# Attention of a hybrid encoder: sample values by pairs, a new split of the copies of turned weights, and a shorter opening

## The chip, the cores and the metric

The kernel runs on one core of one Trainium2 chip. The metric is the device time of one execution in microseconds (us). The core has a matrix engine (TensorE, called PE in the profile), a vector engine (VectorE, DVE), a scalar engine (ScalarE, ACT), a general engine (GpSimd, POOL) and a queue engine (SyncE, SP) that here only issues transfers. Matmuls write into PSUM banks, from which VectorE and ScalarE read. Every engine works through its own list of instructions in order; where one needs another's result, it waits.

## The reference

Two layers over 640 tokens: one new stream of 512 frames (the prompt) and eight running streams with 16 new frames each (the samples). All data are float32. A layer is a gated feed-forward step, a mixer (short convolution and attention from one common projection, merged by two gates) and a second feed-forward step.

```python
x += 0.5 * swiglu(rmsnorm(x, norm_ffn1), w_ffn1_gu, w_ffn1_down)
z = rmsnorm(x, norm_mix) @ w_in            # conv B, C, V | q, k, v | two gates
y_conv = B * causal_conv3(C * V)
y_attn = softmax(q k^T / 8 + rel_bias, banded by chunks of 64) v     # 8 heads of 64
m = sigmoid(g_c) * (y_conv @ w_conv_out) + sigmoid(g_a) * (y_attn @ w_attn_out)
x += m @ w_o
x += 0.5 * swiglu(rmsnorm(x, norm_ffn2), w_ffn2_gu, w_ffn2_down)
```

For the prompt the attention is 512 by 512, with the part above the diagonal of chunks left out. For each sample the 16 new frames read 256 cached keys and values and their own 16. The outputs are the final norm of all tokens and the new keys, values and convolution rows.

## The kernel before

Activations lie with channels on the partitions and 640 tokens along the free axis, in two halves of 320. Each float32 product of a weight matrix is three matmuls of 320 columns: weights and activations are split into a rounded part (whi, hhi, thi) and the rest (wlo, hlo, tlo), and hi x hi, hi x lo and lo x hi are summed in PSUM. The weights stream in as tiles of 512 KB (raw, by SyncE); ScalarE casts each to whi, VectorE subtracts to get wlo, and three buffers of each kind go round.

The opening of the first feed-forward step (`opening`, L620) begins with `stir`: matmuls of a constant tile (ones) whose result nobody reads. TensorE runs them while the first tokens and weights arrive. Each of them has float32 operands and leaves two rows in the trace.

In `attention` the products that turn queries, keys, gates and convolution inputs out of h are handed out as a stream: `fill(n)` runs the next n pieces of it, six matmuls of 320 columns each, and the small matmuls of attention stand between. The prompt's attention takes heads in four passes of two (e = 0 and 1). A pass computes scores (pss), and `softmax` (exponentials on ScalarE, L1943) and `weigh` (scaling on ScalarE, L1801) give the weights. `values` then transposes them on TensorE block by block: for each column block j = 0 to 3, and for each of the two heads, the transposes of `turn` (L1814) write a PSUM tile ptp of 512, 384, 256 or 128 columns, and one copy (L1817) moves it to pt in SBUF, on VectorE for e = 0 and on ScalarE for e = 1. Six transposes stand in the second half of each pass: two of j = 2 for each head and one of j = 3 for each.

The samples come after that. `sscores(b)` loads the cached keys (kc), the cached values (vc) and the new values (vn) of sample b by SyncE, has GpSimd add the 16 new keys, and runs the scores on TensorE (spss, L1872) in strips of 32 columns of the array, one strip for each pair of heads. VectorE adds the bias and takes the maximum (L1879) into a box, and softmax follows. `svalues(b)` has three parts: three transposes of the box (sptp, L1895 and L1896) and their copies on ScalarE and VectorE; then the values (spy, L1906), again in strips of 32 columns, first the new ones with 16 rows (vn) and then the cached ones in two blocks of 128 rows (vc), and a scaling on ScalarE (L1908); then one transpose of the result (ptx, L1912). After every fourth sample the collected results are copied to yas. The box of a sample is a tile of the ring "pt", in use from its scores to its ptx; the scores of b + 2 are written while b is being worked on.

What sets the order: each engine takes its instructions as the code is written, except that those under `soon()` are put forward by up to 300 instructions. PSUM tiles made by `att` go round one set of banks, so that a new tile waits until the tile that had its bank has been read.

Of the kernel before, what the change touches and what calls it, by code (L numbers as in the profile page):

```python
# [10 lines left out]
F32 = mybir.dt.float32  # L11
F32R = mybir.dt.float32r
AF = mybir.ActivationFunctionType
# [167 lines left out]
def trunk(ctx: ExitStack, tc: tile.TileContext, xin, xtok, wst, small, pbias, samplebias, kcache, vcache,  # L181
# [27 lines left out]
    def att(name):  # L209
        return banks["att"].tile([P, 512], F32, tag="att", name=name)  # L210
# [154 lines left out]
    def soon():  # L365
        return tc.high_priority(offset=300)
# [42 lines left out]
    def stir(ps, n):  # L409
        for _ in range(n):  # L410
            PE.matmul(ps[:, :P], ones, ones, start=True, stop=True)
# [203 lines left out]
    def opening(fp, name, goff, n, put, tails):  # L615
# [1 line left out]


        ACT.copy(early, epst)
        stir(att(f"stir{name}"), 15)  # L620
        ex = Expand(fp, name, goff)
        ex.ps = fp.tile([P, NT], F32, name=f"sums{name}", bufs=1)
        load(2)
# [1060 lines left out]
    def attention(l, h, norms, stats, ops, mp, yas, ycp, both, others):  # L1684
# [119 lines left out]
        def values(p):  # L1804

            pt = [mp.tile([P, offs[-1] + SEQ], F32, name=f"pt{l}_{2 * p + e}", tag="pt") for e in range(2)]
            at = [sum(P * (NQ - i) for i in range(j)) for j in range(NQ)]

            def turn(j, e):
                w = (NQ - j) * P  # L1810
                s = weights[2 * p + e]
                ptp = att(f"ptp{l}_{2 * p + e}_{j}")[:, :w]
                for i in range(j, NQ):
                    PE.transpose(ptp[:, (i - j) * P : (i - j + 1) * P],  # L1814
                                 s[:, offs[i] + j * P : offs[i] + (j + 1) * P], ident)
                with soon():
                    (ACT.copy if e else DVE.tensor_copy)(pt[e][:, at[j] : at[j] + w], ptp)  # L1817

            for j in range(NQ):
                for e in range(2):  # L1820
                    turn(j, e)
                if j % 2:
                    yield
            py = att(f"py{l}_{p}")
            for j in range(NQ):
                for e in range(2):
                    hh = 2 * p + e
                    PE.matmul(py[e * HD : (e + 1) * HD, j * P :], vs[j][:, hh * HD : (hh + 1) * HD],
                              pt[e][:, at[j] : at[j] + (NQ - j) * P], start=j == 0, stop=j == NQ - 1)
            ACT.copy(yas[:, p, 0:SEQ], py)  # L1830
            yield
# [17 lines left out]

        sbias = mp.tile([P, KS], F32, name=f"sbias{l}", bufs=1)  # L1850
        POOL.dma_start(sbias, samplebias[l])
        G = 4
        held, ptx = {}, [None]

        def sscores(b):
            n = f"{l}_{b}"
            kcs = []
            for e, tag in enumerate("qk"):
                kc = mp.tile([P, T], F32, name=f"kc{n}_{e}", tag=tag)
                kcs.append(kc[:, : npair // 2 * KS].rearrange("p (a k) -> p a k", k=KS))  # L1860
                SP.dma_start(kcs[e][:, :, :PAST], kcache[l, b, :, e * npair // 2 : (e + 1) * npair // 2])
            vraw = mp.tile([P, offs[-1] + SEQ], F32, name=f"vc{n}", tag="s")
            vraw = vraw[:, : 2 * AW].rearrange("p (a k) -> p a k", a=2)
            SP.dma_start(vraw, vcache[l, b])
            rows = slice(b * TS, (b + 1) * TS)
            vn = mp.tile([P, SEQ], F32, name=f"vn{n}", tag="bias")[:TS, :AW]
            SP.dma_start(vn, vnew[rows])
            for e, kc in enumerate(kcs):
                POOL.tensor_copy(kc[:, :, PAST:], ks[:, e * npair // 2 : (e + 1) * npair // 2, rows])
            pss = att(f"spss{n}")[:, :KS]  # L1870
            for p in range(npair):
                PE.matmul(pss[32 * p : 32 * p + 32], bd[:, b, p, :], kcs[2 * p // npair][:, p % (npair // 2), :],  # L1872
                          start=True, stop=True)

            box = mp.tile([P, offs[-1] + SEQ], F32, name=f"ss{n}", tag="pt")
            s = box[:, :KS]
            st = mp.tile([P, 4, NQ], F32, name=f"sst{n}", tag="st", bufs=4)
            with soon():
                DVE.tensor_tensor_reduce(out=s, in0=pss, in1=sbias, scale=1.0, scalar=NEG,  # L1879
                                         op0=ALU.add, op1=ALU.max, accum_out=st[:, 0, 0:1])  # L1880

                softmax(s, st, [(0, KS)])
                if b == NB - 1:
                    ACT.activation(early, st[:, 3, 0:1], AF.Sigmoid)
            held[b] = box, st, vraw, vn

        def svalues(b):
            n = f"{l}_{b}"
            box, st, vraw, vn = held[b]
            s = box[:, :KS]  # L1890
            pt = box[:, KS : KS + 2 * P].rearrange("p (a b) -> p a b", a=2)
            pn, yx = (box[:n, KS + o * P : KS + (o + 1) * P] for n, o in ((TS, 2), (P, 3)))
            ptp = att(f"sptp{n}")
            for j in range(2):
                PE.transpose(ptp[:, j * P : (j + 1) * P], s[:, j * P : (j + 1) * P], ident)  # L1895
            PE.transpose(ptp[:TS, 2 * P : 3 * P], s[:, PAST:], ident)  # L1896
            with soon():
                ACT.copy(pt, ptp[:, : 2 * P].rearrange("p (a b) -> p a b", a=2))
                DVE.tensor_copy(pn, ptp[:TS, 2 * P : 3 * P])
            yield  # L1900

            pys = att(f"spy{n}")[:, :P]
            for j, (w, v) in enumerate(((pn, vn), (pt[:, 0], vraw[:, 0]), (pt[:, 1], vraw[:, 1]))):
                for p in range(npair):
                    r = slice(32 * p, 32 * p + 32)
                    PE.matmul(pys[r], w[:, r], v[:, p * P : (p + 1) * P], start=j == 0, stop=j == 2)  # L1906
            with soon():
                ACT.activation(yx, pys, AF.Copy, scale=st[:, 3, 0:1])  # L1908
            yield
            if b % G == 0:  # L1910
                ptx[0] = att(f"ptx{n}")
            PE.transpose(ptx[0][:, (b % G) * P : (b % G + 1) * P], yx, ident)  # L1912
            if b % G == G - 1:
                c0 = SEQ + (b + 1 - G) * TS
                for e in range(2):
                    r = slice(e * HD, (e + 1) * HD)
                    with soon():
                        (ACT.copy if e else DVE.tensor_copy)(
                            yas[r, :, c0 : c0 + G * TS].rearrange("p a (b t) -> p a b t", b=G),
                            ptx[0][r].rearrange("p (b a e t) -> p a b e t", b=G, a=npair, e=2)[:, :, :, e, :])  # L1920

        sscores(0)
        sscores(1)
        for b in range(NB):
            vals = svalues(b)
            fill(4)
            next(vals)
            fill(3)
            if b + 2 < NB:
                sscores(b + 2)  # L1930
            next(vals)
            fill(2)
            next(vals, None)
        fill(KT * KT)

    def softmax(s, st, parts):
# [307 lines left out]
```

## Time and profile before

| | |
|---|---|
| median of 3 runs | 2493.01 us (2492.5 to 2493.15) |
| profiled execution | 2492.73 us, its span 2490.9 us |
| granted TensorE clock, mean | 0.999 |
| PE busy | 2481.3 us |
| DVE busy | 2115.8 us |
| ACT busy | 1443.3 us |
| POOL busy | 370.3 us |
| HBM | 223.75 MB read, 7.94 MB written |

The profile is of one execution. Busy times are of each engine, and a share is against the span. In a timeline row the first number is the start in us from the start of the span, the second the length of the group, then engine, source line, operation, what it writes and reads, its form and how many instructions were merged into the row; a bracket names an idle time ahead of it and what ended it. The start of one row to the start of the next is the step in which the engine moves on; the length of a matmul is longer than its step, since matmuls overlap. The prompt's and the samples' attention of layer 0 lie between about 490 and 640 us, those of layer 1 about 1232 us later.

### The profile page before, as it was taken

How to read it: one execution, taken by the hardware profiler on the slowest of the kernel's cores; microseconds unless marked ns; L12 is line 12 of the kernel's file. 1: busy time of each engine (PE TensorE's matmuls, PEld its weight loads, DVE VectorE, ACT ScalarE, POOL GpSimd, SP SyncE). 2: the span in 40 equal slices, each digit the busy share in tenths (PEclk: the TensorE clock that was granted, in tenths of full speed). 3: DMA queues.
4: the chain of work that ended last, by engine and by line, in shares of the span. 5: the costliest groups of instructions: out<-in, count | busy, mean ns of one | idle time of the engine just before them, and what ended most of it. 6: DMA issues, size and time to landing. Idle time of an engine off the chain costs nothing.

```text
span 2490.9 us, 43594 instructions
## 1 busy us (share of the span) xinstructions
PE 2481.3 (100%) x17084; PEld 2424.0 (97%) x17084; DVE 2115.8 (85%) x3327; ACT 1443.3 (58%) x2340; POOL 370.3 (15%) x445
## 2 busy tenths in 40 slices
PE   9999999999999999999999999999999999999998
PEld 9999999888999999999999999998899999999998
DVE  7789888878888899888798889888788888989887
ACT  6445556664666555555555555556646665555554
POOL 0011211111111011111001111121111110111111
PEclk9999999999999999999999999999999999999999
DMA  5244654335345344555435554643344553454554
GB/s 188 82 115 125 137 136 130 108 106 173 102 111 152 98 117 119 134 135 135 117 92 129 130 130 121 138 119 118 127 151 105 125 140 95 119 133 122 130 136 111
DMA packets 134990, 310.74 MB, mean 125 GB/s; under 512 B 12960, under 2 KB 76832, under 8 KB 134784
## 3 DMA queue, kind: packets, MB, share of 16 engines
q1 hardware_dynamic: 70704, 221.80, 26.4%
q0 software_dynamic: 63360, 85.50, 20.5%
q8 instruction: 134, 2.20, 0.4%
q10 hardware_dynamic: 720, 0.65, 0.1%
q14 instruction: 72, 0.59, 0.1%
HBM read 223.75 MB, written 7.94 MB: 93 GB/s over the span
## 4 chain that ended last, share of the span: by engine, by line
PE 95%; DVE 3%; ACT 2%; issue 0%; DVEq 0%; POOL 0%; ACTq 0%; POOLq 0%
PE pab L395 12%; PE paa L395 11%; PE pcb L395 6%; PE pca L395 6%; PE daa L1077 5%; PE dab L1077 5%; PE po L372 4%; PE qa L395 4%; PE pbb L395 3%; PE pba L395 3%; PE dcb L1077 3%; PE dca L1077 3%; PE poa L372 2%; PE pda L372 2%; PE pv L1737 2%; PE ma_cv L395 2%
## 5 line engine op out<-in xcount | busy, mean ns | idle before, releaser
L310 DVE TENSOR_TENSOR wlo<-raw,whi 128x1024 fp32r<-128x1024 f32 (+1 forms) x582 | 597.7, 1030 | 236.1 <-ACT whi L305 230.7
L305 ACT CAST whi<-raw 128x1024 fp32r<-128x1024 f32 (+1 forms) x582 | 518.7, 896 | 350.0 <-PE pbb L395 44.3
L305 ACT CAST whi<-s 128x1024 fp32r<-128x1024 f32 (+1 forms) x164 | 153.4, 936 | 249.3 <-issue 107.8
L395 PE MATMUL pab<-xhib,whi 128*128 128x320 f32 x704 | 218.2, 310 | 0.4 <-DVE gb L249 0.4
L395 PE MATMUL pab<-xhib,wlo 128*128 128x320 f32 x704 | 217.3, 309 | 0.0
L395 PE MATMUL pab<-xlob,whi 128*128 128x320 f32 x704 | 217.3, 309 | 0.0
L395 PE MATMUL paa<-xhia,whi 128*128 128x320 f32 x640 | 198.1, 310 | 0.2 <-DVE ga L249 0.2
L395 PE MATMUL paa<-xhia,wlo 128*128 128x320 f32 x640 | 197.7, 309 | 0.0
L395 PE MATMUL paa<-xloa,whi 128*128 128x320 f32 x640 | 197.7, 309 | 0.0
L310 DVE TENSOR_TENSOR wlo<-s,whi 128x1024 fp32r<-128x1024 f32 (+1 forms) x164 | 176.8, 1078 | 10.5 <-ACT whi L305 10.5
L395 PEld LDWEIGHTS pab<-xhib,whi 128*128 128x128 f32 x704 | 132.1, 188 | 1.1 <-DVE gb L249 0.9
L395 PEld LDWEIGHTS pab<-xlob,whi 128*128 128x128 f32 x704 | 132.1, 188 | 0.2
L395 PEld LDWEIGHTS pab<-xhib,wlo 128*128 128x128 f32 x704 | 132.1, 188 | 0.0
L395 PEld LDWEIGHTS paa<-xhia,whi 128*128 128x128 f32 x640 | 120.2, 188 | 0.5 <-DVE ga L249 0.5
L395 PEld LDWEIGHTS paa<-xloa,whi 128*128 128x128 f32 x640 | 120.2, 188 | 0.1
L395 PEld LDWEIGHTS paa<-xhia,wlo 128*128 128x128 f32 x640 | 120.2, 188 | 0.0
L249 DVE TENSOR_TENSOR raw<-raw,raw 128x512 f32<-128x512 f32 x164 | 112.2, 684 | 1.6
L249 DVE TENSOR_TENSOR raw<-s,raw 128x512 f32<-128x512 f32 x164 | 112.4, 686 | 0.0
L1101 POOL DMA_DIRECT2D x<-c_b x52 | 62.6, 1203 | 310.8 <-ACT c_b L1094 134.5
L395 PE MATMUL pcb<-xhib,whi 128*128 128x320 f32 x352 | 108.7, 309 | 0.0
L395 PE MATMUL pcb<-xlob,whi 128*128 128x320 f32 x352 | 108.7, 309 | 0.0
L395 PE MATMUL pcb<-xhib,wlo 128*128 128x320 f32 x352 | 108.7, 309 | 0.0
(846 smaller groups left out, 8173.5 us busy)
## 6 DMA issues: line engine op xcount, KB each, us to landing
raw<-in_wst SPq DMA_DIRECT2D x374, 512.0 KB, 3.6
x<-c_b POOLq DMA_DIRECT2D x52, 320.0 KB, 5.0
x<-c_a POOLq DMA_DIRECT2D x50, 320.0 KB, 5.0
kc<-in_kcache SPq DMA_DIRECT2D x32, 256.0 KB, 3.7
vc<-in_vcache SPq DMA_DIRECT2D x16, 512.0 KB, 4.6
ub<-cbb POOLq DMA_DIRECT2D x42, 160.0 KB, 5.6
ua<-cba POOLq DMA_DIRECT2D x38, 160.0 KB, 5.2
x<-u_a POOLq DMA_DIRECT2D x18, 320.0 KB, 5.1
```

The source lines that it names most:

```text
L249: DVE.tensor_tensor(out=out, in0=a, in1=b, op=ALU.add)
L305: ACT.copy(hi[:, d], src[:, c])
L310: DVE.tensor_tensor(out=lo, in0=src, in1=hi.bitcast(F32), op=ALU.subtract)
L372: PE.matmul(ps[a] if isinstance(ps, list) else ps[:, a, :HT], w, x[:, a * HT : (a + 1) * HT], start=first and j == 0, stop=last and j == 2)
L395: PE.matmul(ps, a, b, start=start and kp == 0 and j == 0, stop=stop and kp == NP - 1 and j == 2, skip_group_check=True)
L1077: PE.matmul(ps[u], w, y, start=start and i == 0 and j == 0, stop=i == 1 and j == 2, skip_group_check=True)
L1101: POOL.dma_start(rows(r, cols), z, accum_op=ALU.add)
L1737: PE.matmul(pv[t], xx[:, t * P : (t + 1) * P], w[:, kk * AW : (kk + 1) * AW], start=c == 0 and kk == 0 and j == 0, stop=c == KT // 2 - 1 a ...
```

## The change

Three edits. The opening of the first step runs 11 stirring matmuls in place of 15. In `turn` VectorE, in place of ScalarE, copies ptp for the second head in the blocks j = 0 and j = 2. And the samples are taken by pairs: two boxes stay for the whole layer, box b % 2, each with two slots of scores, so that sample b + 2 has another slot than sample b; the transposes of both samples stand together, then four fillers, then the scores of the next two, directly behind them the values of both (cached blocks first, new values last, in turn over the two), four fillers, both ptx transposes and their copy (now after every second sample), and ten fillers.

```diff
-        stir(att(f"stir{name}"), 15)
+        stir(att(f"stir{name}"), 11)
...
-                    (ACT.copy if e else DVE.tensor_copy)(pt[e][:, at[j] : at[j] + w], ptp)
+                    (ACT.copy if e and j % 2 else DVE.tensor_copy)(pt[e][:, at[j] : at[j] + w], ptp)
...
-        G = 4
+        G = 2
         held, ptx = {}, [None]
+        boxes = [mp.tile([P, offs[-1] + SEQ], F32, name=f"ss{l}_{i}", tag="pt") for i in range(2)]
...
-            box = mp.tile([P, offs[-1] + SEQ], F32, name=f"ss{n}", tag="pt")
-            s = box[:, :KS]
+            box = boxes[b % 2]
+            at = b // 2 % 2 * KS
+            s = box[:, at : at + KS]
...
+            pys = [att(f"spy{l}_{b}")[:, :P] for b in bs]
+            for js in ((0, 1), (2,)):
+                for b, ps, pt, pn in zip(bs, pys, pts, pns):
+                    vraw, vn = held[b][2:]
+                    for j in js:
+                        w, v = (pn, vn) if j == 2 else (pt[:, j], vraw[:, j])
+                        for p in range(npair):
+                            r = slice(32 * p, 32 * p + 32)
+                            PE.matmul(ps[r], w[:, r], v[:, p * P : (p + 1) * P], start=j == 0, stop=j == 2)
...
         sscores(0)
         sscores(1)
-        for b in range(NB):
-            vals = svalues(b)
-            fill(4)
-            next(vals)
-            fill(3)
-            if b + 2 < NB:
-                sscores(b + 2)
-            next(vals)
-            fill(2)
-            next(vals, None)
+        fill(7)
+        for b in range(0, NB, 2):
+            vals = svalues((b, b + 1))
+            next(vals)
+            fill(4)
+            for c in range(b + 2, min(b + 4, NB)):
+                sscores(c)
+            next(vals)
+            fill(4)
+            next(vals, None)
+            fill(10 if b + 2 < NB else 0)
         fill(KT * KT)
```

First TensorE at the samples, in layer 0. Before, scores of sample 2 and values of sample 0 stand in one block between ordinary matmuls (ma0_b0):

```order
L395 MATMUL ma0_b0_6186<-tlo0_1_4697,whi147_6152 128x320
L395 MATMUL ma0_b0_6186<-thi0_1_4696,wlo147_6153 128x320
L1872 MATMUL spss0_2_6240<-kc0_2_0_6230,bd0_4718 32x272 x2
L1872 MATMUL spss0_2_6240<-kc0_2_1_6232,bd0_4718 32x272 x2
L1906 MATMUL spy0_0_6251<-vn0_0_6106,ss0_0_6115 32x128 x4
L1906 MATMUL spy0_0_6251<-vc0_0_6104,ss0_0_6115 32x128 x8
L395 MATMUL ma0_b0_6186<-thi0_2_4698,whi147_6152 128x320
```

And now, on the same engine, the block of a pair:

```order
L395 MATMUL ma0_b0_6182<-tlo0_1_4693,whi148_6178 128x320
L395 MATMUL ma0_b0_6182<-thi0_1_4692,wlo148_6179 128x320
L1873 MATMUL spss0_2_6275<-kc0_2_0_6265,bd0_4714 32x272 x2
L1873 MATMUL spss0_2_6275<-kc0_2_1_6267,bd0_4714 32x272 x2
L1873 MATMUL spss0_3_6295<-kc0_3_0_6285,bd0_4714 32x272 x2
L1873 MATMUL spss0_3_6295<-kc0_3_1_6287,bd0_4714 32x272 x2
L1911 MATMUL spy0_0_6305<-vc0_0_6102,ss0_0_6096 32x128 x8
L1911 MATMUL spy0_1_6306<-vc0_1_6122,ss0_1_6097 32x128 x8
L1911 MATMUL spy0_0_6305<-vn0_0_6104,ss0_0_6096 32x128 x4
L1911 MATMUL spy0_1_6306<-vn0_1_6124,ss0_1_6097 32x128 x4
L395 MATMUL ma0_b0_6182<-thi0_2_4694,whi148_6178 128x320
```

Scores of sample 3 and values of sample 1 have joined, and the values' new part (vn) moved behind the cached part of both.

Second ScalarE in the second pass of the prompt's attention of layer 0 (pt0_3 is the second head of that pass, ptp0_3_0 to ptp0_3_3 its four blocks, yc0 and st0_4 the next pass's weights). Before:

```order
L839 COPY capsm0_4691<-ma0_qk3_5494 128x320
L1801 ACTIVATE yc0_4693<-yc0_4693,st0_4_5510 128x128
L1801 ACTIVATE yc0_4693<-yc0_4693,st0_4_5510 128x256
L1817 COPY pt0_3_5589<-ptp0_3_0_5596 128x512
L1817 COPY pt0_3_5589<-ptp0_3_1_5607 128x384
L1801 ACTIVATE yc0_4693<-yc0_4693,st0_4_5510 128x384
L1801 ACTIVATE yc0_4693<-yc0_4693,st0_4_5510 128x512
L305 CAST whi138_5643<-raw78_5641 128x1024
```

And now, on ScalarE:

```order
L839 COPY capsm0_4687<-ma0_qk3_5490 128x320
L1801 ACTIVATE yc0_4689<-yc0_4689,st0_4_5506 128x128
L1801 ACTIVATE yc0_4689<-yc0_4689,st0_4_5506 128x256
L1801 ACTIVATE yc0_4689<-yc0_4689,st0_4_5506 128x384
L1817 COPY pt0_3_5585<-ptp0_3_1_5603 128x384
L1801 ACTIVATE yc0_4689<-yc0_4689,st0_4_5506 128x512
L1951 ACTIVATE yc0_4689,st0_5_5510<-yc0_4689,st0_5_5510 128x256
L305 CAST whi138_5639<-raw78_5637 128x1024
```

The copy of 512 columns has left, and the scaling of 384 columns moved ahead of the copy of 384.

Third SyncE's queue at the samples, which issues weight tiles (raw), keys (kc) and values (vc, vn) in one row. Before:

```order
L245 DMA raw83_6146<-in_wst 128x1024
L1864 DMA vc0_0_6104<-in_vcache 128x1024
L245 DMA raw84_6288<-in_wst 128x1024
L1864 DMA vc0_1_6125<-in_vcache 128x1024
L1861 DMA kc0_2_0_6230<-in_kcache 128x2x256
```

And now, on SyncE:

```order
L245 DMA raw83_6142<-in_wst 128x1024
L1865 DMA vc0_0_6102<-in_vcache 128x1024
L1865 DMA vc0_1_6122<-in_vcache 128x1024
L245 DMA raw84_6253<-in_wst 128x1024
L1862 DMA kc0_2_0_6265<-in_kcache 128x2x256
```

The second sample's values moved ahead of the weight tile raw84.

More of the change, by code (lines that the diff above doesn't have):

```diff
@@ L1884, in sscores @@
                     ACT.activation(early, st[:, 3, 0:1], AF.Sigmoid)
[L1885 to L1899, printed above, removed]
-            yield
[L1902 to L1908, printed above, removed]
-            yield
[L1910 to L1920, printed above, removed]
@@ new lines, in sscores, with svalues @@
+            held[b] = s, st, vraw, vn
+        def svalues(bs):
+            pts = [z[:, 2 * KS : 2 * KS + 2 * P].rearrange("p (a b) -> p a b", a=2) for z in boxes]
+            pns, yxs = ([z[:n, 2 * KS + o * P : 2 * KS + (o + 1) * P] for z in boxes] for n, o in ((TS, 2), (P, 3)))
+            for b, pt, pn in zip(bs, pts, pns):
+                s = held[b][0]
+                ptp = att(f"sptp{l}_{b}")
+                for j in range(2):
+                    PE.transpose(ptp[:, j * P : (j + 1) * P], s[:, j * P : (j + 1) * P], ident)
+                PE.transpose(ptp[:TS, 2 * P : 3 * P], s[:, PAST:], ident)
+                with soon():
+                    ACT.copy(pt, ptp[:, : 2 * P].rearrange("p (a b) -> p a b", a=2))
+                    DVE.tensor_copy(pn, ptp[:TS, 2 * P : 3 * P])
+            yield
+            pys = [att(f"spy{l}_{b}")[:, :P] for b in bs]
[7 more added lines that the diff above has]
+                            PE.matmul(ps[r], w[:, r], v[:, p * P : (p + 1) * P], start=j == 0, stop=j == 2)
+            for b, ps, yx in zip(bs, pys, yxs):
+                with soon():
+                    ACT.activation(yx, ps, AF.Copy, scale=held[b][1][:, 3, 0:1])
+            yield
+            for b, yx in zip(bs, yxs):
+                if b % G == 0:
+                    ptx[0] = att(f"ptx{l}_{b}")[:, : G * P]
+                PE.transpose(ptx[0][:, (b % G) * P : (b % G + 1) * P], yx, ident)
+                if b % G == G - 1:
+                    c0 = SEQ + (b + 1 - G) * TS
+                    for e in range(2):
+                        r = slice(e * HD, (e + 1) * HD)
+                        with soon():
+                            (ACT.copy if e else DVE.tensor_copy)(
+                                yas[r, :, c0 : c0 + G * TS].rearrange("p a (b t) -> p a b t", b=G),
+                                ptx[0][r].rearrange("p (b a e t) -> p a b e t", b=G, a=npair, e=2)[:, :, :, e, :])
```

## The prediction, made before the change was run

> **What bounds the kernel now.** I read the page's busy shares and its chain first, then TensorE's waits, then single rows of the three places that the change touches. The lines are the span, the busy share of the engines, the chain that ended last, and from the view of waits the one wait of TensorE's that the change touches.
>
> ```profile
> span 2490.9 us, 43594 instructions
> PE 2481.3 (100%) x17084; PEld 2424.0 (97%) x17084; DVE 2115.8 (85%) x3327; ACT 1443.3 (58%) x2340; POOL 370.3 (15%) x445
> PE 95%; DVE 3%; ACT 2%; issue 0%; DVEq 0%; POOL 0%; ACTq 0%; POOLq 0%
> ...
> PE ptp L1814 <- ACT pt L1817: 0.9, 4, 0.3
> ```
>
> TensorE is the bound, almost without a gap: 95% of the chain is its own, and for ScalarE's copies (pt) it waits in four places, 0.9 us together. An edit can therefore gain by shortening what TensorE issues, or by those four waits; it loses wherever it makes TensorE wait anew. The profiled execution is 2492.73 us, 1.83 us more than its span and 0.28 us below the median 2493.01; I sum against the profiled one and carry the difference over to the median. What a measurement of this kernel can tell from no change is about 0.2%, here 4.99 us.
>
> **Part 1, the opening.** Each stirring matmul leaves two rows, so 15 are 30 rows and 11 are 22. TensorE first, then what the first real matmuls need.
>
> ```profile
> 1.51 0.64 PE L411 MATMUL stira<-ones 128*128 128x128 f32 x2
> 5.78 0.63 PE L411 MATMUL stira<-ones 128*128 128x128 f32 x2
> 6.42 0.63 PE L411 MATMUL stira<-ones 128*128 128x128 f32 x2
> 7.63 0.46 PE L372 MATMUL poa<-hloa,whi 128*128 128x320 f32 x2
> 8.81 0.46 PE L372 MATMUL poa<-hhia,wlo 128*128 128x320 f32 x2
> ...
> 4.95 0.83 ACT L646 ACTIVATE hhia<-x,sm 128x640 fp32r<-128x640 f32 x1 [2.29 <-DMA sm<-in_small]
> 5.15 0.64 DVE L650 CAST whi<-raw 128x256 fp32r<-128x256 f32 x2 [5.15 <-DMA raw<-in_wst]
> 5.82 0.88 DVE L651 SCALAR_TENSOR_TENSOR hloa<-x,sm,hhia 128x640 fp32r<-128x640 f32 x1
> 6.62 0.75 DVE L655 TENSOR_TENSOR wlo<-raw,whi 128x256 fp32r<-128x256 f32 x2
> ```
>
> From 5.78 to 6.42 stand three steps, 0.213 us each; eight rows fewer would be 1.7 us. The row at 1.51 is the second, so the 22nd starts at 1.51 + 20 x 0.213 = 5.78 and the first real matmul can run at 6.0, when hhia (4.95 + 0.83 = 5.78) and whi (5.15 + 0.64 = 5.79) are ready. But the third one reads hloa, ready at 5.82 + 0.88 = 6.70. It started at 7.63, so it can come at most 0.9 us earlier. Then wlo binds: its first half ends near 7.04 (6.62 plus a little over half of the 0.75), and TensorE will ask for it two matmuls after hloa, at about 7.05. From there on eight matmuls take 8.81 - 7.63 = 1.18 us, 0.147 each, and the second wlo (7.37) is ready well ahead. I take -0.85 us. The ends are -1.7 (no operand late) and a loss, which is the rival on the clock below.
>
> **Part 2, the turned weights of the prompt.** Half of ScalarE's copies of the turned softmax weights (blocks of 512 and 256 columns, odd heads) go to VectorE. The rows: TensorE in the second and third of four passes in layer 0, ScalarE and VectorE in the second.
>
> ```profile
> 514.88 0.38 PE L1814 MATMUL ptp<-ident,s 128*128 128x128 f32 x2
> 515.43 0.70 PE L1814 MATMUL ptp<-ident,s 128*128 128x128 f32 x4 [0.17 <-ACT pt L1817]
> 535.04 0.38 PE L1814 MATMUL ptp<-ident,yc 128*128 128x128 f32 x2
> 535.68 0.70 PE L1814 MATMUL ptp<-ident,yc 128*128 128x128 f32 x4 [0.26 <-ACT pt L1817]
> ...
> 514.81 0.94 ACT L1817 COPY pt<-ptp 128x512 f32<-128x512 f32 x2
> 515.65 1.24 ACT L1801 ACTIVATE yc<-yc,st 128x384 f32<-128x384 f32 x2
> ...
> 513.64 1.12 DVE L1817 COPY pt<-ptp 128x512 f32<-128x512 f32 x2
> 515.30 0.42 DVE L1817 COPY pt<-ptp 128x256 f32<-128x256 f32 x1 [0.54 <-PE ptp L1814]
> ...
> L1817 DVE COPY pt<-ptp x32: 278/477/684, 493.5 to 1783.5; 128x512 f32<-128x512 f32 x8, 128x384 f32<-128x384 f32 x8, 128x256 f32<-128x256 f32 x8, 128x128 f32<-128x128 f32 x8
> ```
>
> Two transposes at 0.11 us a step would put the third at 515.10; it stands at 515.43. So the wait costs some 0.33 us there and, with a slow step behind it, about 0.39; in the third pass 0.48. Both layers together hold 2 x (0.39 + 0.48) = 1.74 us: the most that this part can win.
>
> VectorE gains 0.68 + 0.42 = 1.1 us of copies a pass (its longest row and the row of 256). It sat idle 0.54 us before the copy at 515.30 and has nothing on TensorE's path right behind, so the copies find room. The third transpose group now waits for VectorE's 512 copy, which follows the first one: 513.64 + 2 x 0.68 = 515.0, in time for 515.10. What is late next: the fifth group takes the PSUM bank that ScalarE's copy of 384 columns empties, and the order puts the scaling of the next 384 columns ahead of that copy. ScalarE is free at 514.81; the scaling is the shorter share of the 1.24 us, some 0.52, and the copy 0.42 (0.94 less the 512 block's share). It ends at 515.75, where the fifth group in the trace ran near 515.7. ScalarE has been relieved of a 512 copy in the pass before, so it may be a few tenths early. I take 0 for these two passes, +0.1 us for the first, where an exponential is put ahead of ScalarE's copy, and 0 for the last: +0.2 us over both layers. The ends are -1.7 (nothing late in place of the wait) and +1.5 (0.4 us in four of the eight passes).
>
> **Part 3, the samples by pairs.** First the joint block as it stands in the trace, row by row, with narrow windows to part its steps; then the place ahead of the loop where two samples' scores already stand together.
>
> ```profile
> 566.86 0.31 PE L395 MATMUL ma_b<-thi,wlo 128*128 128x320 f32 x1
> 567.10 0.67 PE L1872 MATMUL spss<-kc,bd 128*32 128x272 f32 x8
> 567.69 0.42 PE L1906 MATMUL spy<-vn,ss 16*32 16x128 f32 x8
> 567.83 0.29 PE L1906 MATMUL spy<-vn,ss 16*32 16x128 f32 x4
> 568.04 0.64 PE L1906 MATMUL spy<-vc,ss 128*32 128x128 f32 x16
> 568.29 0.40 PE L1906 MATMUL spy<-vc,ss 128*32 128x128 f32 x8
> 568.40 0.29 PE L1906 MATMUL spy<-vc,ss 128*32 128x128 f32 x4
> 568.62 0.42 PE L395 MATMUL ma_b<-thi,whi 128*128 128x320 f32 x1
> 568.88 0.31 PE L395 MATMUL ma_b<-tlo,whi 128*128 128x320 f32 x1
> ...
> 559.35 1.12 PE L1872 MATMUL spss<-kc,bd 128*32 128x272 f32 x16
> 560.41 0.41 PE L395 MATMUL ma_cv<-thi,whi 128*128 128x320 f32 x1
> ```
>
> Rows come in fours, one for each strip of 32 columns, and each four is one step. From the ordinary matmul at 566.86 to the second one behind the block (568.88) is 2.02 us, made of: into the block 0.24, scores of one sample 0.59, new values (vn) 0.35, cached values (vc) 0.58, out again 0.26. Two ordinary steps of 0.147 lie in it, so a block costs 1.72 us, and two of them 3.45.
>
> The paired block, from the same steps: into it 0.24; four steps of scores 560.41 - 559.35 = 1.06; eight of vc, the first 0.13 (0.25 for the two steps to 568.29, less 0.11), six of 0.11 (568.29 to 568.40), and the last 0.22, which is the step from one shape to the next (568.40 to 568.62, and 567.83 to 568.04 for vn to vc): 1.01; four of vn, 0.13, twice 0.11, and 0.22 out: 0.57; the slow second ordinary step 0.26. That is 3.14, less 0.29: 2.85 us. One pair saves 0.60.
>
> Three pairs a layer have such a block (scores of the next two, values of these two). The fourth has values alone: singly 0.24 + 0.35 + 0.58 + 0.26 - 0.29 = 1.14 each, 2.28 for two; together 0.24 + 1.01 + 0.57 + 0.26 - 0.29 = 1.79; saved 0.49. A layer saves 3 x 0.60 + 0.49 = 2.29 us, two layers 4.6. The transposes (sptp, ptx) merely stand nearer to each other, which I cost at nothing: their number and steps stay. The copies of ptx become four a layer in place of two on ScalarE and on VectorE each; nobody on TensorE reads them until the merge, so they cost nothing. The fillers are the same matmuls in another order. The bounds: -5.5, if merging the transposes wins as well, and -3.5, if the step between two samples' vc costs as much as one between shapes.
>
> This holds only if nothing new is waited for. Values read copies that ScalarE and VectorE make of the turned weights four fillers earlier, 24 matmuls or 3.5 us; the transposes of the results (ptx) come four fillers behind the block, and before them VectorE does two reductions of scores, ScalarE two exponentials and two scalings.
>
> ```profile
> L1879 DVE CUSTOM_DVE_ANT_0 ss<-spss,sbias x16: 421/442/443, 560.2 to 1853.7; 128x272 f32<-128x272 f32 x16
> 571.52 0.53 ACT L1943 ACTIVATE ss<-ss,sst 128x272 f32<-128x272 f32 x1 [1.29 <-DVE sst L1941]
> L1908 ACT ACTIVATE ss<-spy,sst x16: 362/368/371, 568.8 to 1870.9; 128x128 f32<-128x128 f32 x16
>   PE ptx L1912: 4.1, 6
> ```
>
> These are 2 x (0.44 + 0.53 + 0.37) = 2.7 us, with their hand-overs some 3.3 (an estimate) from the end of the scores; values (1.6) and fillers (3.5) take 5.1. The cover is 1.8 us; gone, TensorE would wait at ptx. The last row is VectorE's: the reductions waited for the transpose ptx of two samples earlier, six times, 4.1 us in all, since the scores had to take the box that it read. With two lasting boxes of two slots that wait has no cause left.
>
> **Sum.** -0.85 + 0.2 - 4.6 = -5.25 us: 2487.48 for the execution profiled, 2487.8 against the median. It lies just beyond the 0.2% bound (2488.0).
>
> **Rivals.** *The clock at the start (no change within 0.2%).* The steps of the opening shorten between 6.42 and 7.63: 0.213 for 128 columns before, 0.147 for 320 after, though the granted clock stands at 1.00 even from 3 to 6 us (the row with 325 GB/s below), so that the steps alone show it. With 22 rows TensorE idles or crawls near 6.5, ahead of hloa. If this puts off the fast clock by 2.5 to 5 us, and every real matmul in that time takes twice its 0.147, then 1.25 to 2.5 us are lost, less the 0.85 won: +1.0 in the middle. With parts 2 and 3 as above: 2493.0 + 1.0 + 0.2 - 4.6 = 2489.6. For it: the fast steps come only some 5 us after the first rows. Against it: the idle stretch is 0.15 us, and waits of 0.17 and 0.26 us inside the kernel slow no matmul behind them for longer than one step. [...]
>
> *New waits eat the saving (no change).* If ScalarE's or VectorE's chain to ptx is later than its 1.8 us of cover by half a microsecond in each of eight pairs, or the prompt's passes lose their +1.5, the sum is -5.25 + 4 or so: 2491.8. For it: ScalarE does casts of 1 us between, and in the paired order two samples' work comes at once. Against: the 1.8 us of cover, and VectorE's reductions that no longer wait for ptx.
>
> *The weights come late (slower).* The change puts two samples' value transfers next to one another on SyncE's queue, ahead of weight tiles. In the two rows of stretches the last three numbers are the granted clock, the share of the DMA engines' time and GB/s.
>
> ```profile
> vc<-in_vcache SPq DMA_DIRECT2D x16, 512.0 KB, 4.6
> 3.00:6.00 3.00, 3.00 (x17) 3.00 (x16) 0.77 (x3) 0.83 (x1) 0.26 (x1) 1.00 1.00 325
> 560.00:640.00 80.00, 80.00 (x716) 71.97 (x705) 65.44 (x140) 40.89 (x84) 9.74 (x23) 1.00 0.44 149
> ```
>
> At 325 GB/s, where the opening has all DMA engines busy (share 1.00), 512 KB more ahead of a weight tile are 1.6 us. If TensorE waited that long in all eight pairs, 12.9 us would be added: -5.25 + 12.9 = +7.7, 2500.7. It decides from 10.24 / 8 = 1.28 us a pair. Against it: TensorE was never idle from 560 to 640 while the transfers ran at 149 GB/s and 0.44 of the DMA engines' time, less than half of that.
>
> **Chances.** The sum as worked out, 2486 to 2489.3: 0.62, with its likeliest 2487.8. The clock: 0.08. Waits that eat the saving: 0.17. Slower by the queue or in a like way: 0.13. The range runs from 2485.6 (the sum with 0.9 us of the prompt's waits won and pairs at -5.5) to 2491.8, the second rival. Faster by over 0.2% needs 2488.0: somewhat more than half of the first case, and the cases in which the prompt's waits are won besides, 0.46; within 0.2%, 0.41; slower, 0.13.
>
> **What would show it.** Right: stir ends near 6.2 and hloa's matmul stands near 6.75; one block of 16 score rows, 32 vc rows and 16 vn rows takes 3.14 us between ordinary matmuls, three times a layer; no wait on ptx or spy; VectorE's wait for ptx gone. In the prompt the wait at the third transpose group is gone and a smaller one stands at the fifth. Wrong: steps of 0.29 us in the first real matmuls, a wait of TensorE at ptx, spy or for a weight tile between 556 and 640 us, or a step of over 0.2 us between two samples' vc.

## The result, and the profile after

The changed kernel takes 2485.65 us, median of 8 runs (2485.24 to 2486.58), against 2492.91 us for the kernel before in the same set (8 runs, 2492.19 to 2493.57): 7.26 us less, a ratio of 0.9971 with a 95% interval of 0.9962 to 0.998. That is faster by 0.29%. The forecast was 2487.8, 5.25 us less; the time lies 0.05 us inside the lower edge of its range (2485.6). The interval takes in the forecast's ratio (0.9979) too, so what separates the two is read from the traces, term by term.

The page of the kernel after, its span, busy shares and chain, and then its view of TensorE's waits (line waited for: us in total, times, longest us):

```profile
span 2483.5 us, 43590 instructions
PE 2474.2 (100%) x17076; PEld 2424.1 (98%) x17076; DVE 2121.3 (85%) x3347; ACT 1439.7 (58%) x2328; POOL 361.0 (15%) x445
PE 96%; DVE 2%; ACT 1%; issue 0%; DMA 0%; DVEq 0%; ACTq 0%
...
PE poa L372 <- DVE hloa L651: 0.4, 1, 0.4
PE paa L395 <- DVE ga L249: 0.2, 1, 0.2
```

TensorE is still the bound. The span fell by 7.4 us and TensorE's busy time by 7.1. The wait for ScalarE's copies (pt) is out of the list, and a wait for hloa in the opening is in it. Laying the starts of TensorE's instructions in the two traces beside each other shows where the lead arises: 0.70 us in the opening, 0.42 in each layer's prompt part, 2.72 in each layer's sample part. That is 6.98 us; the rest lies in steps of some hundredths, about 0.09 of it in each layer just behind the samples, which I did not follow further.

The block of a pair in the kernel after, layer 0, one row for each kind of matmul:

```profile
569.60 0.31 PE L395 MATMUL ma_b<-thi,wlo 128*128 128x320 f32 x1
569.84 1.12 PE L1873 MATMUL spss<-kc,bd 128*32 128x272 f32 x16
570.78 1.06 PE L1911 MATMUL spy<-vc,ss 128*32 128x128 f32 x32
571.76 0.64 PE L1911 MATMUL spy<-vn,ss 16*32 16x128 f32 x16
572.33 0.42 PE L395 MATMUL ma_b<-thi,whi 128*128 128x320 f32 x1
572.59 0.31 PE L395 MATMUL ma_b<-tlo,whi 128*128 128x320 f32 x1
```

From 569.60 to 572.59 are 2.99 us, less two ordinary steps 2.70; the prediction had 3.14 and 2.85. The difference is in the scores: 0.94 us (569.84 to 570.78) where 1.06 was expected, and in the cached values, 0.98 for 1.01. The new values (0.57) and both ends (0.24 and 0.26) came as worked out. So did the transposes: the six of a pair cost 0.66 us over their ordinary steps, the three of one sample 0.33 before, so merging them gains nothing.

The prompt in the second pass of layer 0, first TensorE and ScalarE after, then the third pass: its scores with VectorE's keys, and its six transposes. The second block shows the same scores before, and their wait:

```profile
514.32 1.15 PE L1814 MATMUL ptp<-ident,s 128*128 128x128 f32 x6
515.23 0.40 PE L395 MATMUL ma_qk<-thi,whi 128*128 128x320 f32 x1
...
514.01 0.61 ACT L1801 ACTIVATE yc<-yc,st 128x384 f32<-128x384 f32 x1
514.52 0.46 ACT L1817 COPY pt<-ptp 128x384 f32<-128x384 f32 x1
...
524.71 0.31 PE L395 MATMUL ma_cv<-hhim,wlo 128*128 128x320 f32 x1
524.95 0.38 PE L1784 MATMUL pss<-k,q 64*128 64x128 f32 x2
...
523.61 0.48 DVE L1264 SCALAR_TENSOR_TENSOR k<-ma_qk,rrm 128x320 f32<-128x320 f32 x1
...
534.22 1.07 PE L1814 MATMUL ptp<-ident,yc 128*128 128x128 f32 x6
535.04 0.39 PE L395 MATMUL ma_cv<-thi,whi 128*128 128x320 f32 x1
```

```profile
525.37 0.31 PE L395 MATMUL ma_cv<-hhim,wlo 128*128 128x320 f32 x1
525.76 0.38 PE L1784 MATMUL pss<-k,q 64*128 64x128 f32 x2
...
525.23 0.48 DVE L1264 SCALAR_TENSOR_TENSOR k<-ma_qk,rrm 128x320 f32<-128x320 f32 x1
...
  DVE k L1264: 1.1, 4
```

The six transposes take 0.91 us to the next ordinary matmul, against 1.01 before (514.88 to 515.89): the third no longer waits, and the fifth starts late, at 515.03, when ScalarE's copy that began at 514.52 is through. In the third pass the six take 0.82 us (534.22 to 535.04) against 1.10 before (535.04 to 536.14), and the fifth starts 0.19 late. And a second wait is gone that I had not seen in the trace of before: the scores of the third pass stood 0.39 us behind the ordinary matmul ahead of them, because the scaling of the keys on VectorE (525.23 + 0.48) was just ending, and stand 0.24 behind it now, with the keys ready 0.86 us ahead of their use (523.61 + 0.48). The last row is from the view of the scores' tile (pss) before: TensorE's weight loads sat idle for the keys 1.1 us, four times. The view of waits had left these out.

### The profile page after: what moved, and what is told of

The parts are those of the page before. It is cut to its first block, busy times and chain, and to the rows that moved or that the text cites. A ratio compares the mean times of both kernels' runs of the same rounds, so it can differ in the third digit from the quotient of the medians.

```text
span 2483.5 us, 43590 instructions
## 1 busy us (share of the span) xinstructions
PE 2474.2 (100%) x17076; PEld 2424.1 (98%) x17076; DVE 2121.3 (85%) x3347; ACT 1439.7 (58%) x2328; POOL 361.0 (15%) x445
## 4 chain that ended last, share of the span: by engine, by line
PE 96%; DVE 2%; ACT 1%; issue 0%; DMA 0%; DVEq 0%; ACTq 0%
PE pab L395 12%; PE paa L395 11%; PE pcb L395 6%; PE pca L395 6%; PE daa L1077 5%; PE dab L1077 5%; PE po L372 4%; PE qa L395 4%; PE pbb L395 3%; PE pba L395 3%; PE dcb L1077 3%; PE dca L1077 3%; PE ma_cv L395 2%; PE poa L372 2%; PE pda L372 2%; PE pv L1737 2%
```

## The experiments

Times are medians of several runs, with the kernel before timed on the same chip beside them: 2493.1 for the first four, 2493.2 for the next four, 2493.46 for the last four. The interval of each ratio reaches 2 to 3 us to either side, so a difference of less than that between two medians decides nothing alone; it is read together with the rows.

### The three parts alone

11 stirring matmuls in the kernel before:

```diff
-        stir(att(f"stir{name}"), 15)
+        stir(att(f"stir{name}"), 11)
```

> The kernel before with 11 stirring matmuls and nothing else changed. By the trace of the changed kernel the opening ends up 0.70 us ahead, after the wait for hloa and two slow steps, and nothing later gives it back: 2492.9 - 0.7 = 2492.2 us, and the trace shows the first feed-forward step 0.7 us early throughout. Rival, that the opening's lead is lost at a later wait for weights: 2492.9, and the lead shrinks to zero before the end.

2492.92 us, 0.18 less; ratio 0.9999 (0.999 to 1.0008). Its trace is 0.70 us ahead after the opening, as expected, and still 0.60 at the end. That trace is of the fastest of its eleven runs (2492.10), 0.82 us below their median, so its lead is not the kernel's mean; the section on the opening shows how far single traces differ there.

The copies of turned weights alone:

```diff
-                    (ACT.copy if e else DVE.tensor_copy)(pt[e][:, at[j] : at[j] + w], ptp)
+                    (ACT.copy if e and j % 2 else DVE.tensor_copy)(pt[e][:, at[j] : at[j] + w], ptp)
```

> The kernel before with the copies of turned weights split anew and nothing else changed. By the trace of the changed kernel each layer's prompt part gains 0.42 us: the third transpose group no longer waits (0.39 and 0.48 us in two passes), the fifth group waits in three passes instead, and the scores of the third pass no longer wait 0.16 us for the keys. Sum -0.84: 2492.1 us. Rival, the prediction's term: +0.2, 2493.1 us, if the gain seen came from the other two edits moving the engines' phases.

2492.33 us, 0.77 less; ratio 0.9996 (0.9987 to 1.0005). The interval takes in no change, so the time alone decides nothing. The trace does: the lead grows by 0.44 us over layer 0's passes and by 0.43 over layer 1's, in the same places as in the changed kernel. The gain is this edit's own.

The pairs alone: the changed kernel with 15 stirring matmuls and the old copies.

```diff
+        stir(att(f"stir{name}"), 15)
...
+                    (ACT.copy if e else DVE.tensor_copy)(pt[e][:, at[j] : at[j] + w], ptp)
```

> The kernel before with the samples taken by pairs and nothing else changed. By the trace of the changed kernel the sample part costs 14.63 us a layer over its ordinary matmuls where it cost 17.35, so -2.72 a layer, -5.44 in both: 2487.5 us, with a joint block of a pair at 2.70 us. Rival, the prediction's term: -4.6, 2488.3 us, with a joint block of 2.85 us.

2487.74 us, 5.36 less; ratio 0.9978 (0.9969 to 0.9987). Joint blocks of 2.69 us, 14.63 a layer: the expected 5.44, not the predicted 4.6. Yet with its 15 stirring matmuls this trace, too, is 0.58 us ahead of before's behind the opening. So the moment at which the opening gets through is partly chance.

The three gains add to 0.18 + 0.77 + 5.36 = 6.3 us, 0.9 less than the changed kernel's 7.26 in its first set and 0.6 less than the 6.88 of its second (below); differences of that size the intervals do not resolve.

### Why the block is shorter than worked out

In the changed kernel, the new values back between scores and cached values:

```diff
-            for js in ((0, 1), (2,)):
+            for js in ((2,), (0, 1)):
...
-                            PE.matmul(ps[r], w[:, r], v[:, p * P : (p + 1) * P], start=j == 0, stop=j == 2)
+                            PE.matmul(ps[r], w[:, r], v[:, p * P : (p + 1) * P], start=j == 2, stop=j == 1)
```

> The changed kernel with the new values (vn, 16 rows) of both samples put between the scores and the cached values, where they stood before. Theory: scores (128 rows by 32 columns) and cached values (the same) are one shape to the array, and only a step between shapes is slow; the old order has two such steps inside the block where the new one has one. Then each of the six joint blocks grows by 0.34 - 0.23 = 0.11 us at the end of the scores and by 0.13 - 0.11 at the first cached value, 0.14 in all, and the time by 0.8 us to 2486.5. Rival: the step from scores to values is slow or fast by the operands' own sizes, whatever the shape; then the block keeps its 2.70 us and the time its 2485.65.

```profile
570.07 0.31 PE L395 MATMUL ma_b<-thi,wlo 128*128 128x320 f32 x1
570.31 1.12 PE L1873 MATMUL spss<-kc,bd 128*32 128x272 f32 x16
571.36 0.64 PE L1911 MATMUL spy<-vn,ss 16*32 16x128 f32 x16
571.93 1.08 PE L1911 MATMUL spy<-vc,ss 128*32 128x128 f32 x32
572.94 0.42 PE L395 MATMUL ma_b<-thi,whi 128*128 128x320 f32 x1
573.20 0.31 PE L395 MATMUL ma_b<-tlo,whi 128*128 128x320 f32 x1
```

The block takes 3.13 us, 2.84 over its ordinary steps: 0.14 more, as expected, and within 0.01 of what the prediction had for the other order. The scores take 1.05 us (570.31 to 571.36) where they took 0.94. The time is 2487.32, ratio 0.9976 (0.9967 to 0.9986), 1.0 us above the changed kernel's second set; the blocks account for 0.8 of it.

And the reverse, the kernel before with its samples one by one and the cached values first:

```diff
-            for j, (w, v) in enumerate(((pn, vn), (pt[:, 0], vraw[:, 0]), (pt[:, 1], vraw[:, 1]))):
+            for j, (w, v) in enumerate(((pt[:, 0], vraw[:, 0]), (pt[:, 1], vraw[:, 1]), (pn, vn))):
```

> The kernel before, samples one by one, with the cached values put ahead of the new ones and nothing else changed. If scores and cached values are one shape, each of the 12 joint blocks saves 0.11 us at the end of the scores and 0.03 at the first cached value: 1.72 becomes 1.58 us, 1.7 us in all, 2491.4. Rival: the order matters only with two samples in a block; then 1.72 stays, 2493.1.

```profile
567.03 0.31 PE L395 MATMUL ma_b<-thi,wlo 128*128 128x320 f32 x1
567.26 0.67 PE L1872 MATMUL spss<-kc,bd 128*32 128x272 f32 x8
567.75 0.62 PE L1906 MATMUL spy<-vc,ss 128*32 128x128 f32 x16
568.30 0.42 PE L1906 MATMUL spy<-vn,ss 16*32 16x128 f32 x8
568.65 0.42 PE L395 MATMUL ma_b<-thi,whi 128*128 128x320 f32 x1
568.90 0.31 PE L395 MATMUL ma_b<-tlo,whi 128*128 128x320 f32 x1
```

1.87 us from end to end, 1.58 over the ordinary steps, where it was 1.72; the scores 0.49 where they were 0.59. The time is 2491.91, 1.55 less; its ratio of 0.9993 (0.9985 to 1.0002) does not exclude no change, but the blocks repeat to 0.01 us. So the order within the block is worth 1.7 us without any pairing, and pairing on top of it the other 3.8 of the sample part's 5.44; taken the other way round, pairing in the old order is worth 4.6 and the new order 0.84 on top. The form column of the rows (rows*columns of TensorE's array that a matmul takes) accounts for it: scores and cached values are both 128*32, new values 16*32, ordinary matmuls 128*128. A step from one of these forms to the next costs about 0.11 us beyond the step within one (0.34 against 0.23 at the end of the scores, 0.22 against 0.11 at the end of the cached values), and the first step in the new form 0.02 more (0.13 against 0.11). The two experiments put one change of form less at 0.14 us a block here; what takes the time in such a change they do not show.

### The opening and the clock

The changed kernel once more:

> The changed kernel once more, on the chip of the three kernels beside it. If the moment at which the opening's steps turn fast is chance (in the six traces so far 5.3 to 7.0 us), it lies elsewhere than at 5.5 us again, while the sample and prompt parts repeat to a hundredth; the time is 2485.7 plus or minus 0.5. If the moment follows from the kernel, it is 5.5 again.

2486.32 us (2485.85 to 2487.34), ratio 0.9973 (0.9962 to 0.9984). The steps turned fast at 5.3 us here, 5.5 in the first trace (there from 0.213 us a row of the stirring matmuls to 0.112): by itself that looks like the kernel's own. Over all traces it does not. With 15 stirring matmuls the first fast step stands at 4.7, 5.5, 6.2, 6.35, 6.4, 7.0 (the kernel before) and 7.4 us. The moment when the first matmul on hloa starts follows it; the rows are of the pairs alone and of the single samples with cached values first (15 stirring matmuls each), and of the changed kernel's second trace:

```profile
6.94 0.51 PE L372 MATMUL poa<-hloa,whi 128*128 128x320 f32 x2
```

```profile
7.83 0.45 PE L372 MATMUL poa<-hloa,whi 128*128 128x320 f32 x2
```

```profile
6.89 0.42 PE L372 MATMUL poa<-hloa,whi 128*128 128x320 f32 x1 [0.36 <-DVE hloa L651]
```

With 15 it lies anywhere from 6.88 to 7.83, 7.3 on the mean of seven traces; with 11 or 13 it lies from 6.76 to 6.89, 6.8 on the mean of six, held by hloa. The shorter opening is thus worth 0.5 us on the mean, between nothing and 1.1 in one execution, and the trace on which I worked it out was one of the late ones. At 20 us, behind the opening's slow steps and waits, 0.4 us of the 0.5 are left: there the six traces lie ahead of the trace of before by 0.58 on the mean, and the seven, that one among them, by 0.21.

The second trace also lists a wait that the first did not:

```profile
PE qa L395 <- ACT g L1444: 0.6, 2, 0.4
```

The wait is in every trace, and only its size varies. In the two traces of the result TensorE idles there for 0.12 to 0.14 us in each layer, too short to be listed among its waits; in the list of its weight loads both have the same row:

```profile
PEld qa L395 <- ACT g L1444: 0.8, 2, 0.4
```

Over both layers TensorE idles there 0.25 us in the first trace of the changed kernel, 0.59 in the second, 0.27 before, and 0.40 to 0.83 in the other experiments. That it varies in one and the same kernel is shown; what sets it is open. It may be part of why the single parts do not add up to the whole, which is not shown.

The changed kernel with 15 stirring matmuls again:

> The changed kernel with 15 stirring matmuls again. Theory from the kernel with 11 alone (0.18 us by the medians): the shorter opening is worth 0.2 us, so 2485.9. If the three parts simply add up from the kernels that had one each, 0.77 + 5.36 gives 2487.0 here. The prediction's term for the opening, 0.85, would give 2486.5.

2486.92 us, ratio 0.9974 (0.9963 to 0.9984): 0.6 above the changed kernel timed beside it, between the two theories' 0.2 and 0.85, and near the sum of the parts (2487.0). Its trace turned fast at 4.7 us, and hloa was already the bound (6.88).

13 in place of 11:

```diff
-        stir(att(f"stir{name}"), 11)
+        stir(att(f"stir{name}"), 13)
```

> The changed kernel with 13 stirring matmuls, between the 11 and the 15 tried. They end near 6.3 us with slow steps, and hloa is ready at 6.75 to 6.9 either way, so TensorE idles less and nothing real starts later, unless the clock turns fast late: 2485.7 to 2486.4 as with 11. If the shorter opening were worth 0.85 by its length, 13 would be 0.4 slower than 11.

2486.7 us, 6.8 below the kernel before beside it, as the 11 were 6.9 below theirs in the second set; ratio 0.9973 (0.9962 to 0.9984). No difference from 11 that can be measured.

And 4:

```diff
-        stir(att(f"stir{name}"), 11)
+        stir(att(f"stir{name}"), 4)
```

> The changed kernel with 4 stirring matmuls in place of 11. They end near 2.9 us and TensorE is idle for some 3 us until the first real matmul, near 5.85. Theory: the clock needs work before it turns fast, so the real matmuls begin with steps of 0.29 us and stay so for 2.5 to 5 us, which costs 1.2 to 2.5 us less what they hide in the wait for hloa: 2486.9 to 2488. Rival: the clock turns fast at about the same moment whatever TensorE does; then nothing changes, 2485.7.

```profile
1.14 2.07 PE L411 MATMUL stira<-ones 128*128 128x128 f32 x8 [1.14 <-POOL ones L404]
5.72 0.90 PE L372 MATMUL poa<-hhia,whi 128*128 128x320 f32 x2 [2.50 <-ACT hhia L646]
...
11.14 0.73 PE L372 MATMUL poa<-xhia,whi 128*128 128x320 f32 x2
11.67 0.63 PE L372 MATMUL poa<-xloa,whi 128*128 128x320 f32 x2
...
12.43 0.46 PE L372 MATMUL poa<-hhia,whi 128*128 128x320 f32 x2
```

2487.73 us, 1.4 above the changed kernel. The trace, of the slowest of its ten runs (2489.32), is 2.3 us behind that of the changed kernel by 31 us. Two matmuls take 0.53 us (11.14 to 11.67, where the next pair starts), 0.267 a step, until about 12.1 us, and 0.147 from there. So the real matmuls do run slow behind four stirring matmuls and 2.5 us of idle time, for 6.4 us in this trace; whether the short work or the idle time is to blame one run cannot tell apart. The loss that the clock rival of the prediction feared can thus occur; that it is the clock that makes the steps slow was not shown. With 11 stirring matmuls the slow steps were kept off the real ones, though not by much: in the trace with the new values first the stirring steps were slow to their end, and the first real step took 0.42 us where the other traces with 11 or 13 have 0.25. It cost nothing there, since hloa was ready only at 6.71 and its matmul started at 6.76.

### The prompt: which copy counts

The kernel before with block 0 alone moved to VectorE:

```diff
-                    (ACT.copy if e else DVE.tensor_copy)(pt[e][:, at[j] : at[j] + w], ptp)
+                    (ACT.copy if e and j else DVE.tensor_copy)(pt[e][:, at[j] : at[j] + w], ptp)
```

> The kernel before with VectorE copying the odd head's block 0 (512 columns) alone. Theory: taking 0.57 us off ScalarE at this place is what counts. Then the third transpose group's wait (0.39 and 0.48 us in passes two and three) is gone, the fifth group is late instead by 0.2 to 0.3, and the scores of the third pass no longer wait 0.16 for the keys: 0.25 to 0.42 us a layer. Rival: the 256-column block, which freed the way for the copy of the convolution's part (c), is what counts for the scores: then their wait of 0.16 stays.

```profile
515.41 0.60 PE L1814 MATMUL ptp<-ident,s 128*128 128x128 f32 x4
516.46 0.44 PE L1814 MATMUL ptp<-ident,s 128*128 128x128 f32 x2 [0.44 <-ACT pt L1817]
516.65 0.40 PE L395 MATMUL ma_qk<-thi,whi 128*128 128x320 f32 x1
```

This is one run (2493.83 us), read by its rows alone, as is the next one. The third group's wait is gone, but the fifth now starts 1.05 us behind the first, 0.6 late (four steps of 0.11 would be 0.44). Six transposes take 1.24 us where they took 1.01. The scores of the third pass no longer wait, but those of the second do (0.37 us behind the ordinary matmul in place of 0.25). Over layer 0's passes this loses 0.03 us; the expected gain of 0.25 to 0.42 did not come, since the fifth group's wait was mis-sized and these scores' wait not expected.

Block 2 alone (`e and j != 2`):

> The kernel before with VectorE copying the odd head's block 2 (256 columns) alone. Theory: the third transpose group still waits for ScalarE's copy of block 0 (0.39 and 0.48 us), and the scores of the third pass still wait, since ScalarE is relieved only after the place. Rival: the wait of the scores is gone because the copy of c comes ahead in ScalarE's queue; then 0.16 us a layer.

```profile
PE ptp L1814 <- ACT pt L1817: 0.5, 2, 0.3
PE pss L1784 <- DVE k L1264: 0.4, 2, 0.2
...
534.92 0.92 PE L1814 MATMUL ptp<-ident,yc 128*128 128x128 f32 x6
535.60 0.39 PE L395 MATMUL ma_cv<-thi,whi 128*128 128x320 f32 x1
...
523.34 0.69 DVE L310 TENSOR_TENSOR wlo<-s,whi 128x512 fp32r<-128x512 f32 x1 [0.29 <-ACT whi L305]
530.40 0.40 ACT L1943 ACTIVATE s<-s,st 128x128 f32<-128x128 f32 x1 [4.22 <-DVE st L1941]
```

The last two rows are VectorE's and ScalarE's on the way to the third pass's transposes; before, they were:

```profile
523.88 0.69 DVE L310 TENSOR_TENSOR wlo<-s,whi 128x512 fp32r<-128x512 f32 x1 [0.91 <-ACT whi L305]
530.94 0.40 ACT L1943 ACTIVATE s<-s,st 128x128 f32<-128x128 f32 x1 [4.80 <-DVE st L1941]
```

My theory fell here (one run, 2492.49 us). The third pass's six transposes take 0.68 us, almost without a wait, with ScalarE still copying block 0; and the wait of the third pass's scores is gone with block 2 as well as with block 0. What is left is the second pass's wait (0.3 in each layer) and a new one for the keys of that pass. Over the passes of layer 0 this gains 0.23 us. In the third pass the relief comes by way of VectorE. ScalarE's cast (whi) ends earlier, and VectorE waits 0.29 us for it in place of 0.91; so the row maxima (st), for which ScalarE has sat idle over 4 us in both traces, come earlier. ScalarE's first exponential then stands 1.23 us ahead of the first transpose of this pass (530.40 to 531.63) where it stood 0.81 (530.94 to 531.75), and its copy of block 0 is done in time. In the second pass the same edit leaves the exponential 0.81 us ahead (510.74 to 511.55), and the wait stays, though ScalarE has lost a copy in the pass before as well. So what counts is not which copy ScalarE still has at the place, nor any relief in the pass before, but whether VectorE's maxima come earlier for it; why they do not in the second pass is open. Both blocks together gain 0.44, more than the sum of the two.

VectorE with blocks 0 and 1 in the changed kernel (`e and j > 1` stays with ScalarE):

> The changed kernel with VectorE copying the odd head's blocks 0 and 1 (512 and 384 columns) and ScalarE blocks 2 and 3. If the late step of the fifth transpose group (0.28 us late in the second pass, 0.20 in the third) comes from ScalarE's copy of 384 columns behind a scaling, it is gone, and the sixth group waits for VectorE's fourth copy instead, by about 0.3 us in the same passes: no change within 0.4 us. If it comes from VectorE, the fifth group stays late and the sixth adds to it: +0.5 a layer, 2486.7.

2487.17 us, 0.85 above the changed kernel beside it; ratio 0.9976 (0.9966 to 0.9986). In the second pass the fifth group is 0.10 late where it was 0.28, in the first and third not at all; the sixth is late by 0.36 in the second pass and by 0.14 and 0.13 in the first and third. So the fifth group's lateness was ScalarE's, as the prediction said. The prompt's passes of both layers together lose about 0.35 us against the changed kernel's trace, and layer 0's samples another 0.3, in two long steps at 618 us where TensorE's weight loads wait for ScalarE's copy c; the rest of the 0.85 I did not trace.

## Why the prediction was right, and where not

- **Direction, bound and range** held, the range by 0.05 us. Its lower end was worked out from pairs at -5.5 and the prompt's waits won; both came nearly so, but the -5.5 for another reason than the one given, since merging the transposes won nothing. No new wait came at ptx, at spy or for weights between 556 and 640 us, so the second rival and the slower one were rightly behind. VectorE's wait for ptx is gone.
- **Pairs, -4.6 forecast, -5.44 measured.** The mechanism was right and the term mis-sized. The failing step is "four steps of scores 560.41 - 559.35 = 1.06; eight of vc, the first 0.13": both numbers were read where a step between forms lies (scores to ordinary matmuls, new values to cached ones). Between scores and cached values the form stays, so the last step of the scores is 0.23 and not 0.34, and the first cached value's 0.11. Together that is 0.15 a block (1.06 to 0.94 for the scores, 1.01 to 0.98 for the cached values) and 0.9 us in six blocks.
- **Prompt, +0.2 forecast, -0.84 measured by the trace, -0.77 by the medians of the part alone.** "I take 0 for these two passes" failed in the third pass, where the six transposes take 0.82 us in place of 1.10, the fifth group's new wait being that much shorter than the wait removed; the second pass (-0.09) and the first (+0.13) were right. And a term was missing: the scores of the third pass waited 0.14 to 0.16 us for keys that a relieved ScalarE now lets VectorE finish in time.
- **Opening, -0.85 forecast; -0.70 between the two traces of the result, -0.4 on the mean of all traces, -0.2 to -0.6 by the medians.** The bound by hloa was right, to 0.01 us (6.76, forecast 6.75). What failed was taking the one trace of before for the kernel's mean: it was a late one. Two slow steps behind hloa (6.76 to 7.01 and 7.16 to 7.35) took 0.15 us more.
- **The clock rival** got its slow steps shown by 4 stirring matmuls, and not its condition: the idle 0.36 us ahead of hloa did not bring them back (the three steps behind it took 0.25, 0.145 and 0.19 us). Its 2.5 to 5 us of delay were my estimate, which no trace of before shows; the one run with slow real steps had them for 6.4 us, at 1.8 times 0.147. That the clock sets them stayed unshown.

## What to carry to other kernels

Read the form column (rows*columns of the array) before costing a regrouping of small matmuls: a change of form has its own price (about 0.11 us a step here), so put groups of one form next to each other, and take a step's length from a place with the same forms on both sides. The moment at which the steps of a start turn fast is not to be taken from one trace (4.3 to 7.4 us over the traces here); take several executions before counting its tenths. When work is taken off an engine, list all that it holds up later in the same stage, down to the steps that are 0.1 to 0.2 us long and that no view of waits names.

## What the runs showed of the hardware beyond what I expected

The moment at which TensorE's steps turn fast (in the trace of before from 0.213 to 0.112 us a row of the stirring matmuls) varied from 4.3 to 7.4 us over the executions of kernels that start it alike at 1.14 us and keep it busy with 11 to 15 stirring matmuls; the granted clock, 1.00 in every stretch of the opening of before, showed nothing of the turn in that trace. Behind four stirring matmuls and an idle stretch of 2.5 us, in one trace, real matmuls ran at 0.267 us a step, 1.8 times their 0.147, for 6.4 us.
